# Ranking a kernel's planned instruction orders by due times instead of by place in the text

## The chip, the cores and the metric

The kernel runs on one core of one Trainium2 chip. The metric is the device time of one execution in microseconds (us), as the median of several runs. A core has a matrix engine (TensorE, PE in the profile; its weight loads are PEld), VectorE (DVE), ScalarE (ACT), GpSimd (POOL), and SyncE (SP), which here issues nearly all DMA transfers. Each engine works through a queue of its own, and waits between engines are semaphores.

## The reference

Two transformer layers over 512 latent tokens with 256 context tokens ahead of them, width 1024, all in float32. Layer 0 is a differential attention (two softmaxes per head, one subtracted from the other), layer 1 a grouped-query attention with RMS norms on queries and keys.

```python
for i in range(DEPTH):                       # DEPTH = 2
    shift, scale, gate = adaln(c, ada_w[i], ada_b[i])
    cshift, cscale, cgate = adaln(c_ctx, ada_w[i], ada_b[i])
    h  = rms_norm(x,  pre_g[i]) * (1.0 + scale)  + shift
    hc = rms_norm(xc, pre_g[i]) * (1.0 + cscale) + cshift
    if i % 2 == 0:
        y, yc = diff_attention_mixer(h, hc, a_w_in[j], w_out[i], ...)
    else:
        y, yc = gqa_mixer(h, hc, b_w_in[j], w_out[i], ...)
    x = x + gate * rms_norm(y, post_g[i])
    if not last:
        xc = xc + cgate * rms_norm(yc, post_g[i])
return x
```

Inside a mixer: `q, k, v, z = split(h @ w_in)`, axial rotary positions on the latent tokens, softmax attention of latent queries over latent and context keys, then `(o * silu(z)) @ w_out`.

## The kernel before

Every float32 product is made of three matmuls on a rounded high part and a low part: weights are loaded as `raw`, cast by ScalarE to `whi`, and the rest `wlo = raw - whi` is made in pieces by GpSimd or VectorE; the same is done for activations (`h`), queries and keys (`qh`, `ql`, `kh`, `kl`) and attention weights (`ah`, `al`).

An attention unit is one block of 128 queries of one head. Its scores go to a PSUM tile `sc`; VectorE takes the maximum (`sm<-sc`), ScalarE the exponential with the row sum, GpSimd scales the row (`pp<-pp,sm`). Two units share a tile `pp`. Transposing it takes a VectorE transpose of 32 x 32 blocks and a round trip through DRAM, both issued on SP (`turn`, lines 241 to 253): one write `dr<-pp` of 768 KB, then four reads `at<-dr` of 192 KB. ScalarE and VectorE split `at` into `ah` and `al`, and TensorE multiplies these with `v` into one of four PSUM banks `bk`. There are 16 such round trips in each layer. Projections of later heads (`bk<-h,whi`, `bk<-whi,h`) are the filling between the steps of the attention. The gate of layer 1 is summed up in `gacc` and finished in two halves, `gate<-bk,raw`, with a load of `ada_b` and one of `post_g` into `raw` for each.

The order of the instructions is not the order in which they stand in the program. The kernel's text is run twice. The first time it runs into a `Plan`, which records every call as an `Op` with its engine, its price (`price`, multiplied by `MARGIN = 1.08` on ScalarE, VectorE and GpSimd), its predecessors (`preds`) and the operations that it must merely not overtake (`soft`). `Plan.schedule(rank)` is a list scheduler: it walks along the time, with one simulated clock for each engine. For each engine it looks at the operations whose predecessors are done, finds the earliest time at which one could start, and of all that can start at that time takes the one with the smallest rank. It gives each operation a planned start and end. The second time the text runs into `Emit`, which makes the real instructions, and `Emit.chain` ties the instructions of each engine into the planned order. On the chip each queue then runs in that order, and the semaphores decide when; an instruction whose input is late holds up all that stand behind it on its engine.

The rank of the kernel before is `op.prio`: the operation's number in the text, less an offset that the text sets for urgent steps (`HOT0`, `HOT1`, `HOT`, `RUN`, `WARM`). The window is `AHEAD_OPS = 1500` operations.

A DMA's planned landing was, for every size,

```python
go = s + (570 if op.cost == 196608 else 450)
dma = max(dma, go + 300) + op.cost / 350.0
end = max(go + 1700 + op.cost / 350.0, dma) + (800 if op.cost == 131072 else 300) + DPAD
```

with `op.cost` in bytes, times in ns, and `dma` the planned time at which the transfers so far are through. 196608 bytes is one read `at<-dr`, 786432 one write `dr<-pp`, 131072 the swap `sw<-qr` of layer 0, and 524288 one weight load.

Of the kernel before, what the change touches and what calls it, by code (L numbers as in the profile page):

```python
# [16 lines left out]
D = 1024  # L17
# [30 lines left out]
WBUFS = 3  # L48
MEM = 227168
AHEAD_OPS = 1500  # L50
MARGIN = 1.08
DPAD = 1000
SLOT = {}
XE = [2, 2, 2, 2, 3, 3]
NWARM = 17
# [33 lines left out]
    return ap.bitcast(F32)  # L89


class Op:
    __slots__ = ("n", "eng", "meth", "args", "kw", "prio", "kind", "cost", "outs", "ins", "preds", "soft", "succ", "left", "head", "next", "ready", "start", "end")


QUEUE = {"tensor": "PE", "scalar": "ACT", "vector": "DVE", "gpsimd": "POOL", "sync": "SP"}
# [17 lines left out]
class Plan:  # L114
# [66 lines left out]
    def add(self, q, meth, args, kw):  # L181
        op = Op()
        op.n, op.eng, op.meth, op.args, op.kw = len(self.ops), q, meth, args, kw
        op.prio = op.n - self.offs[-1]
        op.next, op.head = None, op
        self.ops.append(op)
        if self.sizes is None:
            return op
        aps = [a for a in args if isinstance(a, bass.AP)]
        outs, ins = aps[:1], aps[1:]  # L190
        for k, v in kw.items():
            if isinstance(v, bass.AP):
                (outs if k in ("out", "accum_out") else ins).append(v)
        op.preds, op.soft = set(), set()
        fresh = []
        for aps_, w in ((ins, 0), (outs, 1)):
            for ap in aps_:
                far = ap.space == bass.MemoryType.DRAM
                if far and all(ap.tensor.name != d.tensor.name for d in self.drams):
                    continue  # L200
                name, spans, parts = (ap.tensor.name, [(0, 2048)], 1) if far else self.places(ap)
                if name not in self.banks and not far:
                    at = spans[0][0]
                    p = next(p for p in self.pools if p.open and p.base <= at < p.base + p.size)
                    p.users.add(op)
                    if p.mark is not None:
                        op.preds.add(p.mark)
                    held = p.held[max(lo for lo in p.held if lo <= at)]
                    ring = held[0]
                    held[2].add(op)  # L210
                    op.preds |= held[3]
                    if held[1] is None:
                        held[1] = len(ring)
                        ring.append(op)
                    if held[1] and ring[held[1] - 1] is not op:
                        op.soft.add(ring[held[1] - 1])
                if w and q == "PE":
                    spans = [(0, self.banks[name] * 4)]
                for lo, hi in spans:
                    for pg in self.pages(name, lo, hi):  # L220
                        keep = []
                        for h in self.seen.get((name, pg), ()):
                            hop, hlo, hhi, hp, hw = h
                            meet = hlo < hi and lo < hhi and hp & parts
                            if hop is not op and ((w or hw) and meet or name in self.banks and hop.eng != q):
                                op.preds.add(hop)
                            if meet and w and (lo <= hlo and hi >= hhi or name not in self.banks and lo <= max(hlo, pg * 2048) and hi >= min(hhi, pg * 2048 + 2048)) and not hp & ~parts:
                                continue
                            keep.append(h)
                        self.seen[name, pg] = keep  # L230
                    fresh.append((name, lo, hi, parts, w))
        for name, lo, hi, parts, w in fresh:
            for pg in self.pages(name, lo, hi):
                self.seen.setdefault((name, pg), []).append((op, lo, hi, parts, w))
        self.price(op, outs, ins)
        if self.tail is not None:
            op.head = self.tail.head
            self.tail.next = op
            op.soft.add(self.tail)
            op.head.preds |= {p for p in op.preds if p.head is not op.head}  # L240
            op.head.soft |= {p for p in op.soft if p.head is not op.head}
        return op
# [11 lines left out]
    def price(self, op, outs, ins):  # L254
        q, n = op.eng, free_size(outs[0])
        big = max([n] + [free_size(a) for a in ins])
        ps = [a.tensor.name in self.banks for a in ins]
        op.kind = None
        if op.meth == "dma_start":
            op.kind, k = "D", 4  # L260
            for d in outs[0].shape:
                k *= d
            op.cost = k
        elif q == "PE":
            if op.meth == "transpose":
                op.kind, op.cost = "T", 109
            elif outs[0].shape[0] == 32:
                op.kind, op.cost = "A", 436 if n == 512 else 240
            elif ins[0].shape[0] == 64:
                op.kind, op.cost = "S", MMS.get(n, 0.45 * n)  # L270
            else:
                op.kind = "M"
                op.cost = MMS.get(n, 0.45 * n) if ins[0].dtype == F32R else 131 if n <= 8 else 430 if n == 128 else 1.68 * n
        elif q == "ACT":
            func = op.args[2] if op.meth == "activation" else None
            op.cost = 164 + 0.824 * n if any(ps[:1]) else 195 + 0.833 * n
            if "accum_out" in op.kw:
                op.cost += 100
            if func == AF.Identity:
                op.cost += 190  # L280
            elif isinstance(op.kw.get("bias"), bass.AP):
                op.cost += 100
        elif q == "DVE":
            if op.meth == "memset":
                op.cost = 60 + 0.82 * n
            elif op.meth in ("tensor_scalar", "tensor_copy") and not any(ps) and big > 8:
                op.cost = 260 + 0.48 * n
            elif op.meth == "scalar_tensor_tensor" and big > 8:
                op.cost = 180 + 1.0 * n
            else:  # L290
                op.cost = 155 + 1.04 * big
        else:
            if op.meth == "memset":
                op.cost = 100 + 0.82 * n
            elif op.meth == "tensor_scalar":
                op.cost = 190 if n <= 8 else 260 + 0.845 * n
            elif n <= 8:
                op.cost = (560 if n == 1 else 690) if op.args[-1] == ALU.pow else 190
            else:
                op.cost = 190 + 2.155 * n  # L300
        if q in ("DVE", "POOL") and op.kind is None and op.meth not in ("reciprocal", "tensor_reduce", "memset"):
            if not any(ps) and outs[0].tensor.name not in self.banks:
                op.kind = 0.75 if n <= 8 else 0.5 if sum(free_size(a) > 8 for a in ins) >= 2 else 0.25


    def schedule(self, rank):
# [11 lines left out]
        free = dict.fromkeys(SELF, 0.0)  # L318
        hold = {"DVE": 0.0, "POOL": 0.0}
        dma, must, last, run, order, land = 0.0, None, None, 0, [], [0.0] * 8  # L320
        low = 0
        while len(order) < count:
            best = None
            while low < count and ops[low].start is not None:
# [16 lines left out]
            s, op = best  # L341
            e = src = op.eng
            cand[e].discard(op)
            if e == "MARK":
                end = s
            else:
                order.append(op)
            if e == "MARK":
                pass
            elif op.kind == "D":  # L350
                s = max(s, land.pop(0))
                go = s + (570 if op.cost == 196608 else 450)
                dma = max(dma, go + 300) + op.cost / 350.0
                end = max(go + 1700 + op.cost / 350.0, dma) + (800 if op.cost == 131072 else 300) + DPAD
                land.append(end)
                src, free[e] = "DMA", go
            elif e == "PE":
# [17 lines left out]
            else:  # L375
# [4 lines left out]
                end = s + d  # L380
                free[e] = end - ISSUE[e]
            op.start, op.end = s, end
            for o in op.succ:
                if op in o.preds:
                    if e == "MARK":
                        t = end
                    elif o.eng == "MARK":
                        t = end + 40
                    elif src == o.eng:
                        t = s if src == "PE" else end + SELF[src]  # L390
                    else:
                        t = end + HAND.get((src, o.eng), 50)
                    o.ready = max(o.ready, t)
                elif o.eng != e:
                    o.ready = max(o.ready, s + 5)
                o.left -= 1
                if o.left == 0:
                    cand[o.eng].add(o)
        return order


class Emit:
# [1830 lines left out]
```

## Time and profile before

| | |
|---|---|
| median of 3 runs | 790.0 us (789.64 to 793.34) |
| the profiled execution | 789.65 us, its span 787.9 us |
| mean granted TensorE clock | 0.992 |
| TensorE busy | 753.5 us, 96% of the span |
| VectorE, ScalarE, GpSimd busy | 537.2, 482.3 and 458.1 us (68, 61 and 58%) |
| moved by DMA | 128.10 MB, 163 GB/s on average |

All operations carry one line number, 411, because one helper (`Emit.add`) makes them; they are told apart by their tiles, as in `al<-at,ah` (output first). A row of a timeline has the start, the time from the first start to the last end, the engine, the operation with its shapes, the count, and in brackets how long the engine had been idle before it and what ended that. "SPq" is the queue of SyncE, where DMA transfers are issued. The time to landing of a DMA counts from its issue.

### The profile page before, as it was taken

What the parts mean: (1) busy time and instruction counts of PE and PEld (TensorE: products, weight loads), DVE (VectorE), ACT (ScalarE), POOL (GpSimd) and SP (SyncE); (2) the same over time, 40 slices, a digit from 0 to 9 for tenths busy, and PEclk for the clock granted to TensorE, in tenths of its full rate; (3) what the DMA queues carried; (4) which work ended last, traced back from release to release, by engine and by line L of the source; (5) the groups of instructions that cost most, each with busy time, mean ns of one, the idle gap of its engine ahead of it and who ended that gap; (6) DMA issues with size and microseconds to landing.
All of it is one profiled execution on the core that took longest, in us unless ns stands there. A gap on an engine that the chain in (4) does not pass through costs nothing. (4 is left out here: it accounts for less than half of the span.)

```text
span 787.9 us, 14001 instructions
## 1 busy us (share of the span) xinstructions
PE 753.5 (96%) x5098; PEld 662.9 (84%) x5098; DVE 537.2 (68%) x856; ACT 482.3 (61%) x1083; POOL 458.1 (58%) x512
## 2 busy tenths in 40 slices
PE   8899999999999999999999999989999987999997
PEld 6679888878887888787989998889999877788886
DVE  3425679779879768576677754778447787687745
ACT  5624457677576645576657844783467585777742
POOL 4644787797686775668932301446778776563301
PEclk9999999999999999999999999999999999999999
DMA  9961363545564752726636352033437776787613
GB/s 296 363 205 61 114 170 124 148 145 163 170 206 142 220 160 104 218 82 191 212 129 191 113 183 81 25 117 112 131 120 214 197 194 199 198 241 230 174 55 107
DMA packets 64581, 128.10 MB, mean 163 GB/s; under 512 B 6144, under 2 KB 37632, under 8 KB 64512
## 3 DMA queue, kind: packets, MB, share of 16 engines
q1 hardware_dynamic: 61088, 122.06, 50.9%
q10 hardware_dynamic: 3424, 5.15, 2.1%
q8 instruction: 40, 0.66, 0.4%
q14 instruction: 29, 0.24, 0.1%
HBM read 95.72 MB, written 27.26 MB: 156 GB/s over the span
## 5 line engine op out<-in xcount | busy, mean ns | idle before, releaser
L411 PE MATMUL bk<-whi,h 128*128 128x256 f32 (+1 forms) x1184 | 245.9, 300 | 1.8 <-DVE kl L411 0.5
L411 PE MATMUL bk<-h,whi 128*128 128x512 f32 (+2 forms) x832 | 225.1, 351 | 1.4 <-ACT sz L411 0.6
L411 PEld LDWEIGHTS bk<-whi,h 128*128 128x128 f32 x1184 | 191.8, 190 | 14.9 <-issue 5.1
L411 POOL TENSOR_TENSOR wlo<-raw,whi 128x256 fp32r<-128x256 f32 x200 | 166.4, 856 | 44.5 <-ACT whi L411 43.8
L411 PE MATMUL bk<-wlo,h 128*128 128x256 f32 (+1 forms) x592 | 176.7, 299 | 0.7 <-POOL wlo L411 0.5
L411 PEld LDWEIGHTS bk<-h,whi 128*128 128x128 f32 x832 | 143.9, 188 | 22.2 <-issue 7.5
L411 PE MATMUL bk<-h,wlo 128*128 128x512 f32 (+2 forms) x416 | 144.3, 347 | 0.0
L411 PEld LDWEIGHTS bk<-wlo,h 128*128 128x128 f32 x592 | 112.0, 189 | 6.1 <-issue 1.4
L411 DVE TENSOR_REDUCE sm<-sc 128x1 f32<-128x768 f32 (+2 forms) x114 | 101.0, 893 | 19.6 <-PE sc L411 19.4
L411 POOL TENSOR_SCALAR pp<-pp,sm 128x768 f32<-128x768 f32 x64 | 67.3, 1052 | 67.3 <-DVE sm L411 59.3
L411 DVE TENSOR_TENSOR al<-at,ah 128x512 fp32r<-128x512 f32 x96 | 83.2, 887 | 27.3 <-ACT ah L411 26.2
L411 ACT CAST whi<-raw 128x1024 fp32r<-128x1024 f32 (+1 forms) x70 | 71.5, 1022 | 22.9 <-PE bk L411 18.2
L411 PEld LDWEIGHTS bk<-h,wlo 128*128 128x128 f32 x416 | 78.2, 188 | 7.0 <-issue 0.5
L411 ACT CAST ah<-at 128x512 fp32r<-128x512 f32 x96 | 57.4, 619 | 39.4 <-PE bk L411 19.9
L411 DVE STREAM_TRANSPOSE pp<-pp 128x1536 f32<-128x1536 f32 x32 | 56.6, 1769 | 2.8 <-POOL pp L411 2.6
L411 PE MATMUL sc<-qk,qk 64*128 64x384 f32 (+1 forms) x480 | 50.7, 341 | 1.7 <-ACT p L411 1.5
L411 POOL TENSOR_TENSOR sz<-sz,za 128x384 f32<-128x384 f32 (+1 forms) x24 | 29.6, 1237 | 37.6 <-ACT za L411 37.5
L411 ACT ACTIVATE p<-sc,sm 128x768 f32<-128x768 f32 (+1 forms) x64 | 43.8, 688 | 11.2 <-DVE sm L411 7.1
L411 ACT ACTIVATE jk<-bk 128x128 f32<-128x128 f32 (+4 forms) x66 | 22.6, 342 | 45.6 <-PE bk L411 25.5
L411 PEld LDWEIGHTS sc<-qk,qk 64*128 64x128 f32 x480 | 38.2, 184 | 13.1 <-issue 3.3
L411 ACT ACTIVATE pp<-sc,sm 128x768 f32<-128x768 f32 x32 | 28.8, 901 | 29.6 <-DVE sm L411 29.6
L411 DVE RECIPROCAL sm<-sm 128x1 f32<-128x1 f32 (+1 forms) x114 | 17.4, 153 | 41.8 <-ACT p L411 25.1
(198 smaller groups left out, 1422.7 us busy)
## 6 DMA issues: line engine op xcount, KB each, us to landing
dr<-pp SPq DMA_DIRECT2D x32, 768.0 KB, 4.4
at<-dr SPq DMA_DIRECT2D x128, 192.0 KB, 4.6
raw<-in_a_w SPq DMA_DIRECT2D x30, 512.0 KB, 3.8
araw<-in_ada_w SPq DMA_DIRECT2D x12, 1024.0 KB, 6.1
raw<-in_b_w SPq DMA_DIRECT2D x20, 512.0 KB, 3.5
ag<-in_ada_w SPq DMA_DIRECT2D x32, 256.0 KB, 6.5
raw<-in_w_out SPq DMA_DIRECT2D x16, 512.0 KB, 3.8
sw<-qr ACTq DMA_DIRECT2D x32, 128.0 KB, 3.3
```

The source lines that it names most:

```text
L411: self.ops.append(getattr(eng, meth)(*args, **kw))
```

## The change

`Plan.plan` calls `schedule` twelve times. The first time it ranks by `op.prio`. After each time, `latest` walks the operations backwards from the planned end and gives each the latest start (`late`) at which all that depends on it could still keep to its own, with the planned lengths and hand-over times; operations of TensorE must besides fit one behind the other in the order just planned. In the next turn the operations of all engines but TensorE are ranked by `late`; TensorE keeps `op.prio`. Of the twelve plans the one with the earliest planned end is kept.

The planned landings get a rate and a base by size, the issue times 440, 450 and 480 ns, and the padding `DPAD` goes from 1000 to 800 ns. Small ScalarE instructions (up to two elements) are priced 75 ns higher. Two operations of the same engine on one PSUM bank now keep their order of the text (`soft`). `lag` holds the hand-over times that stood in `schedule`, with the same values for operations that depend on one another.

```diff
-DPAD = 1000
+DPAD = 800
+PASSES = 12
+RANKP = ("PE",)
...
                             if hop is not op and ((w or hw) and meet or name in self.banks and hop.eng != q):
                                 op.preds.add(hop)
+                            elif hop is not op and name in self.banks:
+                                op.soft.add(hop)
...
+            if n <= 2 and func is not None:
+                op.cost += 75
...
-                go = s + (570 if op.cost == 196608 else 450)
-                dma = max(dma, go + 300) + op.cost / 350.0
-                end = max(go + 1700 + op.cost / 350.0, dma) + (800 if op.cost == 131072 else 300) + DPAD
+                go = s + (450 if op.cost == 131072 else 480 if op.cost == 196608 else 440)
+                rate, base = {196608: (207, 1450), 786432: (420, 900), 131072: (350, 2500)}.get(op.cost, (350, 1450))
+                dma = max(dma, go + 300) + op.cost / rate
+                end = dma + base - 300 + DPAD
...
+    def plan(self):
+
+        best, rank = None, lambda o: (o.prio, o.n)
+        for i in range(PASSES):
+            order = self.schedule(rank)
+            end = max(o.end for o in order)
+            if best is None or end < best[0]:
+                best = end, order, i
+            self.latest(order, end)
+            rank = lambda o: (o.prio if o.eng in RANKP else o.late, o.n)
+        return best[1]
+
+    def latest(self, order, end):
+        free = dict.fromkeys(SELF, end)
+        for op in reversed(self.seq):
+            t = end - (op.end - op.start)
+            for o in op.succ:
+                t = min(t, o.late - self.lag(op, o))
+            if op.eng == "PE":
+                t = free["PE"] = min(t, free["PE"] - op.occ)
+            op.late = t
...
-        em.chain(pl.schedule(lambda o: o.prio))
+        em.chain(pl.plan())
```

More of the change, by code (lines that the diff above doesn't have):

```diff
@@ L89, in f32 @@
     return ap.bitcast(F32)
+RANKP = ("PE",)
 class Op:
-    __slots__ = ("n", "eng", "meth", "args", "kw", "prio", "kind", "cost", "outs", "ins", "preds", "soft", "succ", "left", "head", "next", "ready", "start", "end")
+    __slots__ = ("n", "eng", "meth", "args", "kw", "prio", "kind", "cost", "outs", "ins", "preds", "soft", "succ", "left", "head", "next", "ready", "start", "end", "occ", "late")
 QUEUE = {"tensor": "PE", "scalar": "ACT", "vector": "DVE", "gpsimd": "POOL", "sync": "SP"}
@@ L320, in schedule @@
         dma, must, last, run, order, land = 0.0, None, None, 0, [], [0.0] * 8
-        low = 0
+        low, self.seq = 0, []
         while len(order) < count:
@@ L343, in schedule @@
             cand[e].discard(op)
+            self.seq.append(op)
             if e == "MARK":
@@ L382, in schedule @@
             op.start, op.end = s, end
+            op.occ = 0 if e == "MARK" else free[e] - s
             for o in op.succ:
[L384 to L395, printed above, removed]
+                o.ready = max(o.ready, s + self.lag(op, o))
                 o.left -= 1
@@ L399, in schedule, with lag @@
         return order
+    def lag(self, op, o):
+        e, d = op.eng, op.end - op.start
+        if op not in o.preds:
+            return 0 if o.eng == e else 5
+        if e == "MARK":
+            return d
+        if o.eng == "MARK":
+            return d + 40
+        src = "DMA" if op.kind == "D" else e
+        if src == o.eng:
+            return 0 if src == "PE" else d + SELF[src]
+        return d + HAND.get((src, o.eng), 50)
+    def plan(self):
[17 more added lines that the diff above has]
+            op.late = t
 class Emit:
```

## Prediction

> **What bounds the kernel now.** I read the page first, then the table of stretches, then the timelines of single engines around the longest idle times of TensorE, and last the DMA groups. The page gives the busy time:
>
> ```profile
> span 787.9 us, 14001 instructions
> PE 753.5 (96%) x5098; PEld 662.9 (84%) x5098; DVE 537.2 (68%) x856; ACT 482.3 (61%) x1083; POOL 458.1 (58%) x512
> ```
>
> TensorE (PE) is without a matmul for 787.9 - 753.5 = 34.4 us. The change keeps every matmul, so that sum, and what a lowered clock costs, is all that an order can win. The table of stretches shows where it lies (columns: stretch in us, its length, then busy us and count of PE, PEld, DVE, ACT and POOL, granted clock, DMA share, GB/s; the last row is the sum of 13 stretches of which I show eight):
>
> ```profile
> 0.00:20.00 20.00, 16.03 (x106) 12.65 (x106) 7.63 (x23) 10.87 (x22) 9.16 (x19) 0.91 0.96 297
> 20.00:40.00 20.00, 17.27 (x116) 13.13 (x117) 9.67 (x17) 12.19 (x22) 12.78 (x18) 1.00 1.08 363
> 520.00:540.00 20.00, 17.03 (x129) 16.35 (x128) 13.76 (x38) 11.39 (x46) 8.49 (x10) 0.91 0.32 94
> 620.00:640.00 20.00, 16.98 (x104) 14.85 (x103) 15.17 (x22) 14.53 (x29) 13.68 (x14) 1.00 0.77 193
> 640.00:660.00 20.00, 16.20 (x116) 14.60 (x114) 16.02 (x21) 13.75 (x33) 14.32 (x18) 1.00 0.79 219
> 660.00:680.00 20.00, 19.22 (x113) 17.73 (x114) 14.06 (x27) 13.93 (x35) 14.51 (x20) 0.91 0.60 162
> 680.00:700.00 20.00, 17.66 (x98) 15.00 (x97) 16.02 (x23) 14.70 (x28) 10.31 (x11) 1.00 0.80 241
> 760.00:788.00 28.00, 22.35 (x144) 20.07 (x142) 13.08 (x21) 7.13 (x20) 3.89 (x14) 0.95 0.28 94
> sum 268.00, PE 239.64 PEld 213.06 DVE 181.65 ACT 162.17 POOL 137.29; mean PE 18.43 PEld 16.39 DVE 13.97 ACT 12.47 POOL 10.56
> ```
>
> The 13 stretches hold 268.00 - 239.64 = 28.4 us of the idle time; the other 520 us hold only 6.0. The first 40 us have 3.97 + 2.73 = 6.7, while the DMA engines are full (0.96 and 1.08). The last stretch has 5.65, nearly all behind the last matmuls. That leaves 34.4 - 6.7 - 5.65 = 22.05 us in between, nearly half of it in the attention of layer 1 (620 to 700: 3.02 + 3.80 + 0.78 + 2.34 = 9.9 in the four rows). No engine is full there. So the waits come from order and latency, which is what this change touches. The longest ones, in brackets (idle us before the instruction, and what ended it):
>
> ```profile
> 256.11 0.51 PE L411 MATMUL bk<-al,vhi 128*128 128x256 f32 x2 [1.98 <-DVE al L411]
> 525.89 0.66 PE L411 MATMUL sc<-ident,gacc 128*128 128x128 f32 x4 [1.10 <-POOL gacc L411]
> 633.13 0.47 PE L411 MATMUL bk<-ah,vh 128*128 128x256 f32 x2 [2.65 <-DVE gate L411]
> 660.32 0.44 PE L411 MATMUL sc<-kh,qh 128*128 128x384 f32 x1 [2.25 <-DVE sm L411]
> 684.21 0.51 PE L411 MATMUL bk<-ah,vh 128*128 128x256 f32 x2 [1.94 <-ACT ah L411]
> ```
>
> These five, 9.92 us, carry the sum.
>
> **What the change does to the plan.** No instruction is added or removed; only the order within each engine's queue differs. Two edits only fix or price things (a bank's readers on one engine keep their text order; ScalarE instructions on up to two elements are planned 75 x 1.08 = 81 ns longer); I cost them at nothing, for both move at most a neighbour of under 1 us on queues that are 58 to 68% busy, as the page's second line shows, and if that cover is gone they cost such a neighbour once.
>
> *The landings.* By the formulas in the code, issue to planned landing of the write `dr<-pp` goes from 450 + 1700 + 2247 + 1300 = 5.70 us to 440 + 300 + 1872 + 600 + 800 = 4.01. A group of four reads `at<-dr`, first issue to last landing, goes from 3 x 570 + 4132 = 5.84 (one read alone: 570 + 1700 + 562 + 1300 = 4132 ns) to 480 + 300 + 4 x 950 + 1150 + 800 = 6.53. A 512 KB weight goes from 4.95 to 4.19. The DMA groups say (KB each, median us to landing; the last line is from the view of the tile `at`):
>
> ```profile
> dr<-pp SPq DMA_DIRECT2D x32, 768.0 KB, 4.4
> at<-dr SPq DMA_DIRECT2D x128, 192.0 KB, 4.6
> raw<-in_a_w SPq DMA_DIRECT2D x30, 512.0 KB, 3.8
> DMA to landing us min/median/max: 2.8/4.6/8.5
> ```
>
> The write was planned 1.3 us too late, and is now 0.4 too early; the reads, planned at 4.13 each, are now at 3.68, 4.15, 4.62 and 5.10, mean 4.39, nearer to 4.6. What that does to SP's in-order queue:
>
> ```profile
> 613.88 0.34 SPq L411 DMA_DIRECT2D dr<-pp  x1
> 619.74 0.35 SPq L411 DMA_DIRECT2D raw<-in_ada_b  x1
> 620.65 2.06 SPq L411 DMA_DIRECT2D at<-dr  x4
> 668.29 0.34 SPq L411 DMA_DIRECT2D dr<-pp  x1
> 673.59 0.35 SPq L411 DMA_DIRECT2D raw<-in_ada_b  x1
> 674.47 2.27 SPq L411 DMA_DIRECT2D at<-dr  x4
> ```
>
> With 5.70 the reads were planned ready at 619.58 and 673.99, about when the bias loads were, and they stand behind them. With 4.01 they are ready at 617.89 and 672.30 and go ahead. By the median of 4.4 the data was there at 618.3 and 672.7, so the reads start 2.3 and 1.8 us sooner. Behind a waiting read on SP stand two bias loads, due only at the gate, and weight loads with a buffer of slack. What the reads release:
>
> ```profile
> 629.77 1.14 ACT L411 CAST ah<-at 128x512 fp32r<-128x512 f32 x2 [2.93 <-DMA at<-dr]
> 630.43 1.29 DVE L411 TENSOR_TENSOR al<-at,ah 128x512 fp32r<-128x512 f32 x2 [2.23 <-ACT ah L411]
> 632.31 0.67 DVE L411 TENSOR_TENSOR gate<-bk,raw 128x512 f32<-128x512 f32 x1
> 683.54 1.14 ACT L411 CAST ah<-at 128x512 fp32r<-128x512 f32 x2 [3.98 <-DMA at<-dr]
> ```
>
> At 633.13 TensorE waited for a bank that the addition into `gate` (ending 632.98) had to empty, and this stood on VectorE behind `al`, which waited 2.23 us for the late read. Reads 2.3 us sooner put `gate` at about 630.0 to 630.7, and a due-time rank puts it ahead of `al` besides: the matmul behind it needs its bank first. Either alone takes nearly all of 2.65. At 684.21 the read itself was late: 1.8 of the 1.94 goes.
>
> *The rank.* Candidates that can start at the same time are now taken by latest start on ScalarE, VectorE, GpSimd and SP; TensorE keeps the old rank. Three waits show an instruction that was in no hurry ahead of one that TensorE stood waiting for:
>
> ```profile
> 254.09 0.94 DVE L411 TENSOR_REDUCE sm<-sc 128x1 f32<-128x768 f32 x1
> 254.94 1.71 DVE L411 TENSOR_TENSOR al<-at,ah 128x512 fp32r<-128x512 f32 x2
> 522.09 2.64 POOL L411 TENSOR_TENSOR wlo<-raw,whi 128x256 fp32r<-128x256 f32 x3 [1.20 <-ACT whi L411]
> 524.72 1.11 POOL L411 TENSOR_SCALAR gacc<-gacc,sm 128x1024 f32<-128x1024 f32 x1
> 656.21 1.77 DVE L411 STREAM_TRANSPOSE pp<-pp 128x1536 f32<-128x1536 f32 x1
> 657.91 0.91 DVE L411 TENSOR_REDUCE sm<-sc 128x1 f32<-128x768 f32 x1
> ```
>
> At 256.11 the maximum ahead of `al` costs 254.94 - 254.09 = 0.85. At 525.89 one of three weight pieces ahead of the scaling of `gacc` could have gone behind it: 2.64 / 3 = 0.88. At 660.32 the transpose ahead of the maximum that empties the score bank costs 1.77 of the 2.25.
>
> *The clock.* The row 660 to 680 has 0.91, (1 - 0.91) x 20 = 1.8 us of matmul time lost, right behind the 2.25 us wait; the row 520 to 540 has the same behind 1.10 and a further short wait. I count the first, 1.8, and not the second, since part of its waits stays. The bounds are 0 and 3.6. The Trainium skill (TensorE: Matmul & The Clock Gate, Part 1) says that the clock halves after an idle window of about 3.4 us, and that this window runs free of the kernel. By its idle rule no wait here would cost clock, and this term would be 0; the rows show the loss behind shorter waits, so the measurement decides, and its free-running window would explain why the 2.65 us wait (row 620 to 640, 1.00) lost none.
>
> *The sum.* 2.65 + 1.80 + 0.85 + 0.88 + 1.77 + 1.8 = 9.75 us. What is put back is late next: the maximum set behind `al` (0.94), and the transpose set behind a maximum (0.91), which delays its round trip through DRAM. I give both back in full: 1.85. That leaves 7.9. The profiled execution took 789.65 us by the times (its span and 1.75 around it), 0.35 under the median of 790.0: 789.65 - 7.9 + 0.35 = 782.1, forecast as 782.
>
> *Costed at nothing, with bounds.* The first 40 us: at the start many loads are ready at once, so the rank by due time can reorder SP's whole list. With the DMA engines full the sum of the loads sets the pace, hence 0; at best the 2.73 idle of the second row goes, at worst one 512 KB load stands wrongly ahead, 524 KB / 363 GB/s = 1.4 us. The tail, 5.65, is one chain behind the last matmul and stays. Were half of the 22.05 - 7.95 = 14.1 us of waits not named above to go as well, and the second clock loss, the time would be 782.1 - 7.05 - 1.8 = 773.2.
>
> **The rivals.**
>
> *Landings planned too early (slower).* Unloaded, a round trip is now planned 11.54 - 10.54 = 1.0 us shorter, though reads landed as late as 8.5 us. In an in-order queue a cast placed for a landing that has not come holds everything behind it, as `al` held `gate` at 630.43. The waits view says how often ScalarE stood so:
>
> ```profile
> ACT ah L411 <- DMA at<-dr: 17.2, 8, 4.0
> ```
>
> If each of the eight waits grows by 1.0 and none of the named gains comes, the time is 790 + 8 = 798. It decides if the added waits come to more than the 9.75. Against it: with a weight load in the queue, one round trip now takes 1.87 + 3.80 + 1.50 = 7.2 us of planned transfer time, where it took 2.25 + 2.25 + 1.50 = 6.0, so under the loads of 620 to 700 (DMA 0.60 to 0.80) landings are planned later, not sooner. The Trainium skill (DMA: Bandwidth & Descriptors, Latency and other measured facts) has the access latency of HBM rise under load, about 0.2 to 2 us. That speaks for this rival, since the new table has constant bases; the spread of 2.8 to 8.5 us agrees.
>
> *Traded waits (no change).* TensorE has 96% and each rescued wait lets other work run out earlier; the attention chain of layer 1, not TensorE, then sets 600 to 720, and new waits of 7.9 us replace the old: 790. For it: 620 to 700 has idle time in every row. Against it: the named waits lie in that very chain.
>
> *The due times are not used.* The plan with the earliest end is kept, and the first of the twelve passes still ranks by text. If that one wins, only the landings act: 2.65 + 1.80 = 4.45, time 785.6.
>
> **How the numbers follow.** A measurement of this kernel can tell a change from none by about 0.5%, 4 us: faster is under 786, slower over 794. The forecast has 0.58, the unused due times 0.06 (just faster), traded waits 0.14, landings too early 0.22: faster 0.64, same 0.14, slower 0.22. The range goes from 773 (half of the other waits too) to 798 (the rival's price). The forecast's own case, which holds most of the chance, is 773 to 786.
>
> **What would show it.** PE's busy time stays near 753 less the clock loss; its idle sum falls from 34.4 to about 27. On SP, reads stand ahead of bias loads around 620 and 674. `gate` stands ahead of `al`, `gacc` ahead of the weight pieces, and the row 660 to 680 has a clock of 1.00. ScalarE's waits for `at` fall below 17.2 us. I am wrong if those grow, if the first 40 us lose more than 1.4, or if the five waits go and the idle sum stays.

## The result and the profile after

The changed kernel takes 771.54 us (median of 6 runs, 771.46 to 771.79), the kernel before 789.82 beside it: a ratio of 0.9765 with a 95% interval of 0.9745 to 0.9784. That is 18.3 us faster, where 7.9 were forecast, and 1.5 us below the range. The direction was right, the size less than half. One execution of e11 and one of e13 below ran at a granted clock of 0.75 and took over 900 us, and are left out of the medians and ratios.

The page of the changed kernel, with the lines that answer to those of before:

```profile
span 769.7 us, 14027 instructions
PE 745.0 (97%) x5098; PEld 658.7 (86%) x5098; DVE 543.3 (71%) x856; ACT 481.4 (63%) x1083; POOL 459.6 (60%) x512
```

TensorE is idle for 769.7 - 745.0 = 24.7 us, 9.7 less than the 34.4 of before. The same 5098 matmuls are also busy 8.5 us less. The span fell by the sum, 18.2.

The table of stretches, with the columns of before:

```profile
0.00:20.00 20.00, 13.87 (x109) 11.13 (x110) 8.69 (x26) 12.22 (x24) 7.95 (x18) 1.00 0.99 307
20.00:40.00 20.00, 18.23 (x125) 15.17 (x124) 7.11 (x14) 10.47 (x18) 10.07 (x16) 0.91 1.08 363
520.00:540.00 20.00, 18.73 (x159) 18.49 (x158) 18.16 (x43) 9.70 (x36) 13.70 (x14) 1.00 0.47 144
620.00:640.00 20.00, 18.12 (x131) 17.05 (x130) 16.53 (x23) 16.07 (x35) 15.45 (x17) 1.00 0.86 261
640.00:660.00 20.00, 18.81 (x128) 17.31 (x128) 15.85 (x29) 12.96 (x35) 17.07 (x21) 1.00 0.67 185
660.00:680.00 20.00, 18.35 (x100) 15.79 (x99) 17.37 (x23) 17.06 (x36) 13.69 (x15) 1.00 0.86 247
680.00:700.00 20.00, 20.00 (x120) 18.06 (x119) 16.79 (x23) 14.33 (x30) 8.33 (x6) 1.00 0.94 253
760.00:770.00 10.00, 4.09 (x35) 3.88 (x33) 5.28 (x10) 1.45 (x6) 0.74 (x2) 0.93 0.51 184
```

The first 40 us have 6.13 + 1.77 = 7.9 us of idle time (6.7 before) and the end 5.9 (5.65 before), so 24.7 - 7.9 - 5.9 = 10.9 are left of the 22.05 in between. The clock is 1.00 in the two stretches in between (520 to 540 and 660 to 680) that had 0.91 before. At the start one stretch still has 0.91, now the second instead of the first.

Where the time went is best read from the first matmul of each stage: the first scores of layer 0 (`sc<-qk,qk`), the first transpose of the normed residual behind layer 0 (`sc<-ident,xn`), the first scores of layer 1 (`sc<-kh,qh`). The views of these tiles give the duration (min/median/max ns) and the first and last start. Before:

```profile
L411 PE MATMUL sc<-qk,qk x480: 274/333/445, 79.8 to 415.6; 64*128 64x384 f32 x128, 64*128 64x256 f32 x32
L411 PE MATMUL sc<-ident,xn x32: 270/272/273, 489.4 to 514.7; 128*128 128x128 f32 x32
L411 PE MATMUL sc<-kh,qh x64: 336/338/517, 573.1 to 721.8; 128*128 128x384 f32 x64
```

After:

```profile
L450 PE MATMUL sc<-qk,qk x480: 275/334/446, 77.6 to 410.4; 64*128 64x384 f32 x128, 64*128 64x256 f32 x32
L450 PE MATMUL sc<-ident,xn x32: 270/272/273, 483.2 to 505.6; 128*128 128x128 f32 x32
L450 PE MATMUL sc<-kh,qh x64: 334/338/445, 561.6 to 701.9; 128*128 128x384 f32 x64
```

The four stages that these starts bound, with the span's end, in us (the other columns are experiments, below):

| stage | before | after | new landings only (e1) | due times on ScalarE only (e10) |
|---|---|---|---|---|
| start | 79.8 | 77.6 | 80.9 | 77.8 |
| layer 0 | 409.6 | 405.6 | 407.1 | 408.5 |
| residual, keys and values of layer 1 | 83.7 | 78.4 | 83.0 | 79.8 |
| attention of layer 1 and the end | 214.8 | 208.1 | 211.1 | 206.4 |
| span | 787.9 | 769.7 | 782.1 | 772.5 |

Each column comes from one profiled execution. So the gain is 2.2 + 4.0 + 5.3 + 6.7 = 18.2 us, and only 6.7 of it lies in the last stage, where the prediction had put nearly all of its own. The starts of e1, whose span is 782.1 us:

```profile
L450 PE MATMUL sc<-qk,qk x480: 276/334/443, 80.9 to 415.3; 64*128 64x384 f32 x128, 64*128 64x256 f32 x32
L450 PE MATMUL sc<-ident,xn x32: 270/272/273, 488.0 to 514.0; 128*128 128x128 f32 x32
L450 PE MATMUL sc<-kh,qh x64: 333/337/525, 571.0 to 709.9; 128*128 128x384 f32 x64
```

The busy times in the same four stages, before and then after, say what the gain is made of:

```profile
0.00:79.80 79.80, 72.91 (x485) 57.75 (x485) 32.85 (x72) 38.36 (x67) 39.50 (x57) 0.98 0.70 230
79.80:489.40 409.60, 403.67 (x2803) 352.38 (x2803) 298.43 (x443) 257.61 (x558) 256.38 (x247) 1.00 0.51 157
489.40:573.10 83.70, 80.21 (x561) 74.22 (x560) 55.00 (x117) 49.54 (x150) 48.47 (x68) 0.98 0.29 91
573.10:787.90 214.80, 196.74 (x1254) 178.55 (x1252) 150.89 (x225) 136.76 (x310) 113.73 (x142) 0.99 0.62 177
0.00:77.60 77.60, 69.69 (x485) 56.79 (x485) 32.66 (x72) 38.00 (x66) 37.80 (x57) 0.98 0.72 240
77.60:483.20 405.60, 403.65 (x2806) 352.51 (x2806) 302.00 (x445) 259.22 (x559) 252.82 (x247) 1.00 0.51 158
483.20:561.60 78.40, 77.01 (x554) 71.51 (x553) 58.15 (x117) 49.29 (x150) 50.27 (x65) 1.00 0.30 97
561.60:769.70 208.10, 194.62 (x1258) 177.93 (x1257) 150.49 (x225) 134.85 (x310) 118.71 (x144) 1.00 0.63 182
```

The stages hold the same matmuls but for seven or fewer. In layer 0 all of the gain is idle time of TensorE (5.9 us before, 2.0 after); its busy time there is the same. At the start the busy time falls by 3.2 us, in the stage of the residual by 3.2 and in the last by 2.1.

The steps that the prediction named are in the trace. On SP, one group of reads now stands ahead of the bias loads, and its round trip goes from issue to issue in 3.5 us:

```profile
598.58 0.34 SPq L450 DMA_DIRECT2D dr<-pp  x1
602.07 1.73 SPq L450 DMA_DIRECT2D at<-dr  x4
603.91 0.37 SPq L450 DMA_DIRECT2D raw<-in_ada_b  x1
```

The addition into `gate` stands ahead of `al`, and `gacc` ahead of the weight's cast and pieces (timelines of VectorE, ScalarE and GpSimd):

```profile
609.79 0.69 DVE L450 TENSOR_TENSOR gate<-bk,raw 128x512 f32<-128x512 f32 x1
610.40 2.18 DVE L450 TENSOR_TENSOR al<-at,ah 128x512 fp32r<-128x512 f32 x2
...
512.87 0.53 ACT L450 ACTIVATE sm<-sm 128x1 f32<-128x1 f32 x2
513.50 1.32 POOL L450 TENSOR_SCALAR gacc<-gacc,sm 128x1024 f32<-128x1024 f32 x1 [2.11 <-ACT sm L450]
514.08 1.04 ACT L450 CAST whi<-raw 128x1024 fp32r<-128x1024 f32 x1
515.20 1.44 POOL L450 TENSOR_TENSOR wlo<-raw,whi 128x256 fp32r<-128x256 f32 x2 [0.38 <-ACT whi L450]
```

The wait of TensorE at `gate`, 2.65 us before, is gone. The longest that are left in the attention of layer 1 are these:

```profile
676.06 0.44 PE L450 MATMUL sc<-kh,qh 128*128 128x384 f32 x1 [1.65 <-ACT pp L450]
637.42 0.50 PE L450 MATMUL bk<-ah,vh 128*128 128x256 f32 x2 [1.12 <-ACT ah L450]
```

### The profile page after: what moved, and what is told of

The parts are those of the page before. It is cut to its first block, busy times and chain, and to the rows that moved or that the text cites. A ratio compares the mean times of both kernels' runs of the same rounds, so it can differ in the third digit from the quotient of the medians.

```text
span 769.7 us, 14027 instructions
## 1 busy us (share of the span) xinstructions
PE 745.0 (97%) x5098; PEld 658.7 (86%) x5098; DVE 543.3 (71%) x856; ACT 481.4 (63%) x1083; POOL 459.6 (60%) x512
## 2 busy tenths in 40 slices
DMA packets 64581, 128.10 MB, mean 166 GB/s; under 512 B 6144, under 2 KB 37632, under 8 KB 64512
## 4 chain that ended last, share of the span: by engine, by line
PE 76%; DMA 7%; DVE 7%; ACT 4%; issue 3%; POOL 2%; SPq 1%; ACTq 0%; DVEq 0%; POOLq 0%
PE bk L450 63%; PE sc L450 14%; DMA ag<-in_ada_w 2%; DMA sw<-qr 1%; DMA araw<-in_ada_w 1%; DVE al L450 1%; DVE pp L450 1%; DVE sm L450 1%; DMA raw<-in_a_w 1%; DMA dr<-pp 1%; SPq L450 1%; DMA xt<-in_x 1%; DVE p L450 1%; DVE sw L450 1%; ACT za L450 1%
## 5 line engine op out<-in xcount | busy, mean ns | idle before, releaser
L450 PE MATMUL bk<-h,whi 128*128 128x512 f32 (+2 forms) x832 | 222.7, 349 | 0.0
L450 POOL TENSOR_TENSOR wlo<-raw,whi 128x256 fp32r<-128x256 f32 x200 | 169.1, 870 | 46.7 <-ACT whi L450 46.4
L450 DVE TENSOR_REDUCE sm<-sc 128x1 f32<-128x768 f32 (+2 forms) x114 | 101.1, 894 | 13.8 <-PE sc L450 11.7
L450 DVE TENSOR_TENSOR al<-at,ah 128x512 fp32r<-128x512 f32 x96 | 88.4, 940 | 26.2 <-ACT ah L450 24.5
L450 DVE SCALAR_TENSOR_TENSOR pp<-p,sm,pp 128x768 f32<-128x768 f32 x32 | 41.7, 1304 | 3.8 <-POOL pp L450 2.5
```

The lines of the kernel that those rows point to most:

```text
L450: self.ops.append(getattr(eng, meth)(*args, **kw))
```

## The experiments

All times are medians, and each ratio is to the kernel before in the same session, with its 95% interval. All kernels compute the whole reference; they differ in the planned order only. The changed kernel is the base unless another is named. The theories are lettered in the expectations: A, the rank by due times makes the gain; B, the corrected landings do.

**e1, the landings without the rank.** One pass, hence the rank by text; landings, price and order of readers as in the change.

```diff
-PASSES = 12
+PASSES = 1
```

> The changed kernel with one pass instead of twelve: the rank stays by place in the text, the new landings, the price of small ScalarE instructions and the order of readers of one bank are in. Theory A (the due-time rank makes the gain, by many short waits on all stages): 786 us, between 781 and 793, PE idle above 30 us. Theory B (the corrected landings make it): 776 us or less. The prediction's own sum for the landings alone is 785.6.

785.04 us, 0.9942 (0.992 to 0.9964): 5.3 less than the 790.37 of its session, where the sum said 4.45. Theory B falls. The views of waits show what the landings do: ScalarE's casts wait for reads for 3.3 us in all, not 17.2.

```profile
ACT ah L450 <- DMA at<-dr: 3.3, 2, 2.0
```

TensorE is still idle for 782.1 - 750.5 = 31.6 us:

```profile
span 782.1 us, 14030 instructions
PE 750.5 (96%) x5098; PEld 663.9 (85%) x5098; DVE 543.7 (70%) x856; ACT 481.4 (62%) x1083; POOL 458.8 (59%) x512
```

Theory A is supported by what is left for the rank: 785.04 - 771.54 = 13.5 us.

**e2, the rank without the landings.** The old landing formula and `DPAD = 1000` back in.

```diff
-                go = s + (450 if op.cost == 131072 else 480 if op.cost == 196608 else 440)
-                rate, base = {196608: (207, 1450), 786432: (420, 900), 131072: (350, 2500)}.get(op.cost, (350, 1450))
-                dma = max(dma, go + 300) + op.cost / rate
-                end = dma + base - 300 + DPAD
+                go = s + (570 if op.cost == 196608 else 450)
+                dma = max(dma, go + 300) + op.cost / 350.0
+                end = max(go + 1700 + op.cost / 350.0, dma) + (800 if op.cost == 131072 else 300) + DPAD
```

> The changed kernel with the old landing formula and padding of 1000: the rank by due times in twelve passes acts alone. Theory A: 774 us (770 to 778), nearly all of the gain. Theory B: 784 or more.

772.78 us, 0.9781 (0.9751 to 0.9811). The rank without the new landings (the price and the order of readers are in) makes 17.6 of the 18.3 us, although ScalarE's waits for reads stay at 14.5 us:

```profile
ACT ah L449 <- DMA at<-dr: 14.5, 7, 3.8
```

So the two gains are not a sum: 5.3 and 17.6 alone, 18.3 together. Whether the landings still give anything once the rank is in, these two do not show: 772.78 and 771.54 us have intervals that overlap.

**e3 and e4, the rank on SP only, and on all but SP.**

```diff
-RANKP = ("PE",)
+RANKP = ("PE", "ACT", "DVE", "POOL")     # e3
+RANKP = ("PE", "SP")                     # e4
```

> The changed kernel, but only SP (the DMA issues) is ranked by due times; ScalarE, VectorE and GpSimd by place in the text. Theory A1 (the order of the three compute engines ends the waits): 785 us, no better than the landings alone. Theory A2 (SP's queue, reads ahead of bias loads, ends them): 776.

> The changed kernel, but SP is ranked by place in the text; ScalarE, VectorE and GpSimd by due times. Theory A1: 773 us (770 to 777). Theory A2: 783 or more.

e3: 784.21 us, 0.9922 (0.9895 to 0.995), what the landings give alone. e4: 768.39 us, 0.9731 (0.9697 to 0.9765). The order of DMA issues by due time brings nothing; that of the compute engines brings it all, and with SP by text the median is 3.2 us below that of the change, though the intervals overlap.

**e5, e6 and e7, the rank on one part of the program.** Two cuts in the text, at the end of layer 0's attention and at layer 1's query projections; due times rank one part, the text the others.

```diff
-            rank = lambda o: (o.prio if o.eng in RANKP else o.late, o.n)
+            rank = self.by_part
...
+DUE = (0,)                               # e5; (1,) in e6, (2,) in e7
...
+    def by_part(self, o):
+        part = sum(o.n >= c for c in self.cuts)
+        if o.eng in RANKP:
+            return o.prio, o.n
+        return part, o.late if part in DUE else o.prio, o.n
```

> New landings; due times rank only the operations of the start and of the attention of layer 0, the rest by text. Against 785.0 of the landings alone. Theory A (each stage has its own gain, and they add up to the 13.5 us between 785.0 and 771.5; by first matmuls of stages in the whole change: 3.3 + 1.4 = 4.7 here): 780 us. Theory C (a wait ended early comes back later, as the landings alone gained 9.3 us in the attention of layer 1 and lost 5.6 behind it): 784 to 785.

> New landings; due times rank only the operations from the output projection of layer 0 to the key and value projections of layer 1. Theory A: 4.7 us less than the landings alone, 780. The prediction's single wait of 0.88 us there: 784. Theory C: 784 to 785.

> New landings; due times rank only the operations from the query projections of layer 1 on. Theory A: 3.1 us less than the landings alone, 782. Theory C: here nothing can come back later but at the end itself, so this part alone gives most: 776 or less.

e5: 776.71 us, 0.9828 (0.9794 to 0.9862). e6: 781.55 us, 0.9878 (0.9846 to 0.991). e7: 781.1 us, 0.9866 (0.9836 to 0.9897). Against the 785.04 of e1 the parts give 8.3, 3.5 and 3.9, together 15.7 where the whole rank gave 13.5. By the ratios, which take out the difference between sessions, they give 9.0, 5.1 and 6.0, together 20.1 beside 14.0; the intervals reach 2.4 to 2.7 us to either side of each part. So theory C, by which the first two parts give next to nothing alone, falls, but that the gains add up exactly is not shown. These kernels also rank every operation of an earlier part ahead of all of a later one, and no run has that alone. The first part is worth the most, 8.3 us, more than the 4.7 expected of it, and the prediction had counted 0.85 there. By the starts it lies in its own stages, the start at 77.1 and layer 0 at 403.3, each 3.8 us shorter than in e1:

```profile
L458 PE MATMUL sc<-qk,qk x480: 274/334/443, 77.1 to 408.6; 64*128 64x384 f32 x128, 64*128 64x256 f32 x32
L458 PE MATMUL sc<-ident,xn x32: 270/272/298, 480.4 to 504.9; 128*128 128x128 f32 x32
```

**e8, one turn instead of eleven.**

```diff
-PASSES = 12
+PASSES = 2
```

> The changed kernel with two passes instead of twelve: the plan is the first one ranked by due times. If the turns matter (the due times of one order do not fit the next): 777 us or more. If the rank alone does it: 771 to 774.

781.69 us, 0.9879 (0.9845 to 0.9913): 10 us slower than with twelve. Its first scores of layer 1 start at 563.9, near the 561.6 of the change, but its last stage takes 782.1 - 563.9 = 218.2 where the change takes 208.1. The turns matter, and most of the loss is in the last stage. That the due times of the first order do not fit the second there is an argument, not shown. Twelve turns also give twelve plans to choose from, and no run tells a better rank from a better choice.

**e9, the price that the prediction costed at nothing.** The kernel before, with one edit.

```diff
+            if n <= 2 and func is not None:
+                op.cost += 75
```

> The kernel before with only the higher price of ScalarE instructions on up to two elements; rank by text, old landings. The prediction cost this at nothing: 790 us within 0.5%. Rival: under a rank by text a price of 81 ns on a softmax chain shifts which operation is ready first often enough to move the time by 4 us or more, either way.

796.24 us beside 790.86, 1.0067 (1.0044 to 1.009): 5.4 us slower. The rival holds. A price that is 81 ns higher, on instructions whose own time does not change, moved the order enough to cost more than any single wait of the five.

**e10, e11 and e12, the rank on one engine.**

```diff
-RANKP = ("PE",)
+RANKP = ("PE", "DVE", "POOL", "SP")      # e10, ScalarE by due times
+RANKP = ("PE", "ACT", "POOL", "SP")      # e11, VectorE
+RANKP = ("PE", "ACT", "DVE", "SP")       # e12, GpSimd
```

> New landings; only ScalarE is ranked by due times, the other queues by text. The prediction's named rank waits lay on VectorE and GpSimd, none on ScalarE: by it 785 us, as the landings alone. Theory D (ScalarE stands nearest ahead of TensorE, empties its banks and casts for it, so that its order decides): 777 us.

> New landings; only VectorE is ranked by due times. The prediction's named waits on VectorE (0.85 and 1.77, with the clock loss of 1.8 behind the second): 781 us, and then most of what a single engine gives. Theory D: 783 or more.

> New landings; only GpSimd is ranked by due times. The prediction's named wait on GpSimd (0.88): 784 us. Theory D: 783 or more. Theory E (the queues share the gain about evenly and it adds up): 780 each for ScalarE, VectorE and GpSimd.

e10: 773.37 us, 0.9774 (0.9741 to 0.9808). e11: 779.41 us, 0.9854 (0.9815 to 0.9894). e12: 784.23 us, 0.9904 (0.987 to 0.9938). Theory D holds for ScalarE, which alone gives 11.7 us; VectorE gives 5.6 (the expectation of e17 has 4.6) and GpSimd 0.8, whose interval overlaps that of e1. In sum this is near the 781 and 784 of the named waits, but by stage it is luck. With its span of 782.2 us, e12 takes 415.3 in layer 0, 8.2 more than e1, and 206.0 in the last stage, 5.1 less:

```profile
L450 PE MATMUL sc<-qk,qk x480: 274/334/579, 78.9 to 424.3; 64*128 64x384 f32 x128, 64*128 64x256 f32 x32
L450 PE MATMUL sc<-ident,xn x32: 270/272/327, 494.2 to 520.1; 128*128 128x128 f32 x32
L450 PE MATMUL sc<-kh,qh x64: 333/338/670, 576.2 to 716.6; 128*128 128x384 f32 x64
```

e11 wins 0.9, 1.9, 1.6 and 1.7 us in the four stages, where 0.85 was named in layer 0 and 1.77 with the clock's 1.8 in the last. All three kernels take twelve turns where e1 takes one; e3 and e12, with 0.8 each, show that turns alone do not bring the gain. The starts of e10's stages, for the last column of the table above, and its busy times:

```profile
L450 PE MATMUL sc<-qk,qk x480: 276/333/443, 77.8 to 406.9; 64*128 64x384 f32 x128, 64*128 64x256 f32 x32
L450 PE MATMUL sc<-ident,xn x32: 270/272/273, 486.3 to 511.2; 128*128 128x128 f32 x32
L450 PE MATMUL sc<-kh,qh x64: 333/338/522, 566.1 to 708.1; 128*128 128x384 f32 x64
PE 748.0 (97%) x5098; PEld 662.7 (86%) x5098; DVE 543.2 (70%) x856; ACT 481.7 (62%) x1083; POOL 457.9 (59%) x512
```

Against e1 it wins 3.1 at the start, 3.2 in the middle and 4.7 in the last stage, and loses 1.4 in layer 0. ScalarE is busy for 481.7 us, as in the kernel before (482.3): it does the same work for the same time, in another order.

**e13 and e14, which ScalarE instructions.** Rank by text, new landings (as e1), and one class of ScalarE instructions moved: those that read a bank `bk` 5000 places ahead, or the casts of streamed weights 6000 places back.

```diff
+        op.bank = q == "ACT" and bool(ins) and "bk" in ins[0].tensor.name
...
-        best, rank = None, lambda o: (o.prio, o.n)
+        best, rank = None, lambda o: (o.prio - (5000 if o.eng != "MARK" and o.bank else 0), o.n)   # e13
...
-        nc.scalar.copy(hi, r)
+        with pl.priority(-6000):                                                                    # e14
+            nc.scalar.copy(hi, r)
```

> Rank by text and new landings (785.0 so far); only ScalarE instructions that read one of the four banks bk, and so empty it for TensorE, are put 5000 places ahead. Theory D1 (TensorE waits for banks whose copies stand behind other work on ScalarE): 776 us or less, most of the 11.7 that ScalarE's due times gave. Theory D2 (it is weight casts and gate work that should go later): 782 or more.

> Rank by text and new landings; only the casts of streamed weights whi<-raw are put 6000 places back. Theory D1: 784 us. Theory D2: 778 or less.

e13: 785.21 us, 0.9936 (0.9916 to 0.9956). e14: 786.33 us, 0.9948 (0.9927 to 0.9969). Neither differs from e1, so theories D1 and D2 both fall as they were tried, with one offset and one turn. That the same copy is urgent in one place and not in the next is an argument, not shown.

**e15 and e16, the price beside the landings and under the rank.** The price edit taken out, in e15 from e1 and in e16 from the change.

```diff
-            if n <= 2 and func is not None:
-                op.cost += 75
```

> Rank by text and new landings, without the higher price of small ScalarE instructions. If the price costs here what it cost alone: 785.0 - 5.4 = 780 us, and the landings are worth about 10, more than twice the term 4.45. If the landings made up for it: 785.

> The whole change without the higher price. If the price only harms the rank by text, since due times count the whole chain either way: 771.5 us within 2. If it costs the same everywhere: 766.

e15: 783.1 us, 0.9899 (0.9851 to 0.9947), against 0.9942 with the price. e16: 768.61 us, 0.9722 (0.9676 to 0.9769), against 0.9765. The differences, 1.9 and 2.9 us, lie between the two expectations, and the intervals of each pair overlap. The 5.4 us of e9 are not found again in full; whether the price costs anything here these two leave open.

**e17 and e18, whether shares add up.** ScalarE and VectorE by due times; and the whole change without the price and with SP by text.

```diff
-RANKP = ("PE",)
+RANKP = ("PE", "POOL", "SP")             # e17
+RANKP = ("PE", "SP")                     # e18, and without:
-            if n <= 2 and func is not None:
-                op.cost += 75
```

> New landings; due times rank ScalarE and VectorE, while GpSimd and SP go by text. If the shares add up: 785.0 - 11.7 - 4.6 = 768.7 us. If the two queues mend the same waits: 773, as ScalarE alone.

> The whole change without the higher price and with SP ranked by text. If the two savings (3.1 and 2.9 us) add up: 765.5 us. If each is only a lucky plan: 768 to 772.

e17: 773.77 us, 0.9803 (0.9774 to 0.9832), no better than ScalarE alone: on the queues the shares overlap. e18: 765.03 us, 0.9692 (0.9664 to 0.972), the fastest kernel here, 6.5 us under the change; its interval ends below that of the change. The two savings added up to what was expected, 765.5, though the interval of e18 overlaps those of e4 (from 0.9697) and e16 (from 0.9676), so neither saving is shown by itself.

## Why the prediction was right or wrong

**The bound.** It failed first here: "that sum, and what a lowered clock costs, is all that an order can win". Idle time gave 9.7, but busy time gave 8.5 with the same matmuls. Two stretches at 0.91 that are now at 1.00 explain 3.6, an estimate of (1 - 0.91) x 20 each. Of the other 4.9 the rows by stage put 3.2 at the start, 1.4 in the stage of the residual and 0.3 in the last. They may be waits that the trace books as busy time, since the page's head says that the ends of matmuls are modelled; no run shows it. The Trainium skill (Trainium Kernel Development and Optimization, Performance Expectations) calls matmul busy time a bad metric because matmuls are pipelined, and names the busy share of weight loads among the good ones. This case agrees in that the same 5098 matmuls were busy for 753.5 and for 745.0 us; the weight loads' busy share went from 84 to 86%, and their sum from 662.9 to 658.7 us.

**The landings.** The sum was right, the account only in part. The term of 4.45 measured 5.3 with the price and the order of readers in it (e1), and 6.8 without the price (e15). The waits for reads fell from 17.2 to 3.3 us. But the last stage, where both waits of this term lay, won 3.7; layer 0, without a term, won 2.5, and the start lost 1.1. In e1 none of the five named waits is over 1.2 us any more, but TensorE waits as long elsewhere, at places where the kernel before has no wait of 1 us:

```profile
527.04 0.40 PE L450 MATMUL bk<-whi,h 128*128 128x256 f32 x1 [2.47 <-DVE kn L450]
616.60 0.33 PE L450 MATMUL bk<-ident,q 128*128 128x128 f32 x1 [2.05 <-POOL q L450]
```

And the term cannot be added to the rank's (e2).

**The rank's terms.** Here the forecast was lost. The rank's part of the sum was 0.85 + 0.88 + 1.77 + 1.8 - 1.85 = 3.45 us; it measured 13.5 on top of the landings and 17.6 without them (e1, e2). The step that failed is "These five, 9.92 us, carry the sum": of what was not named, half was allowed as a bound and nothing in the forecast. The five lay where waits were long, not where they were many. The start was costed at 0 and won 2.2; layer 0 was costed at 0.85, less 0.94 given back, and won 4.0; the stage of the residual was costed at 0.88 and won 5.3, of which 1.8 is the clock loss that I chose not to count. The list of the longest waits had also left one out, longer than the 1.10 that it names just before, which the prediction calls "a further short wait" and gives no term:

```profile
528.26 0.66 PE L411 MATMUL sc<-ident,gacc 128*128 128x128 f32 x4 [1.72 <-ACT hf L411]
```

In the last stage the terms 2.65 + 1.80 + 1.77 + 1.8 less 0.91 are 7.1, and that stage won 6.7. The agreement does not bear them out: without the new landings the 1.80 of the late read falls away, which leaves 5.3, and e2 wins 214.8 - (770.7 - 564.0) = 8.1 us there:

```profile
L449 PE MATMUL sc<-kh,qh x64: 333/337/445, 564.0 to 703.5; 128*128 128x384 f32 x64
```

**The engine.** The three named rank waits lay on VectorE and GpSimd; for these two the totals came out near (e11, e12), but not at the places named. No rank term lay on ScalarE, and its queue alone gives 11.7 us (e10). It casts and copies between TensorE's steps, and a matmul's wait names only its last releaser; that this hid it is an argument. Which of its instructions do it stays open: two classes were tried and neither does (e13, e14). The Trainium skill (TensorE: Matmul & The Clock Gate, Architectural detail) describes ScalarE's and VectorE's queues as strictly first in, first out. No run here tests that; e10 fits it, since reordering one such queue, with 481.7 us of work as before, moved the whole kernel.

**What was given back.** 1.85 was set against the gain. No run isolates that term. That a new order brings losses of its own shows twice: in the new waits of 2.47 and 2.05 us in e1, and in the 8.2 us that layer 0 loses in e12. How much of this the change pays stays open.

**What was costed at nothing.** The price edit was not nothing: 5.4 us alone (e9). Its cover was argued from queues that are 58 to 68% busy; but an order can change at every place where two candidates meet, not once. Beside the rest of the change its cost is not settled (e15, e16). The order of a bank's readers, costed at nothing too, no run isolates.

**The rivals.** Landings planned too early: ScalarE's waits for reads did not grow but fell, 4.7 us in the change:

```profile
ACT ah L450 <- DMA at<-dr: 4.7, 6, 2.0
```

Traded waits: new ones do come (e1, e12), but under the whole rank they do not cancel the gain, and TensorE's idle time falls by 9.7 us. Due times not used: that would be e1, 785.04, and its price of 785.6 was right.

## What to carry to other kernels

Where an engine is 96% busy and waits in many places, do not sum its longest waits: time the stages by their first matmul, and give each stage and each queue a term. Put no price at nothing if a planner reads it. And when a planner gets better ranks, try each queue by itself: here ranking the queue of DMA issues brought nothing, and both kernels without it (e4, e18) had medians some 3 us below those with it (the change, e16).

## What the hardware showed that was not expected

The length of a wait does not decide whether the clock falls. Before, a stretch of 20 us at 0.91 followed a wait of 2.25 us, and another the waits of 1.10 and 1.72; e1 has 0.95 and 0.97 in the stretches around its wait of 2.05. None fell behind the 2.65 us before or the 2.47 in e1. After the change, no stretch of 20 us between 40 and 760 is under 1.00. The DMA groups of the changed kernel (KB each, median us to landing):

```profile
dr<-pp SPq DMA_DIRECT2D x32, 768.0 KB, 4.2
at<-dr SPq DMA_DIRECT2D x128, 192.0 KB, 4.1
```

The median landing of the reads went from 4.6 to 4.1 us and that of the writes from 4.4 to 4.2, with the same 128.10 MB in a shorter time: a table of landings taken from one order does not quite fit the next.
